# Attention stage of a two-layer decoder step: rotation of gathered query rows by pairs of tiles, sinks as a score column, half the keys for the first block

## The chip, the cores and the metric

The kernel runs on one core of a Trainium2 chip. The metric is the device time of one launch, in microseconds. Three runs of the kernel before took 1693.32, 1693.46 and 1696.6 us, with a median of 1693.46 us.

## What is computed

One inference step of a two-layer decoder, for a prompt of 512 tokens and 8 single-token samples (520 columns together), with a width of 1024, in float32. Each layer is a half-weighted SwiGLU, a token mixer, and a second half-weighted SwiGLU. The mixer of layer 0 is a pooling mixer. The mixer of layer 1, which the change touches, is sliding-window attention with 16 query heads, 4 key heads and a head width of 64. The first 16 rows of each head are rotated by position, and each head has a sink, a score that takes part in the softmax but has no value. Cut to what matters:

```
def _rope(x, pos):                       # first 16 of the 64 rows of a head
    out = concat([x1 * cos - x2 * sin, x2 * cos + x1 * sin, x[..., 16:]])

def _sink_attention(q, k, v, mask, sinks):
    s = einsum(q, k) * HEAD_DIM ** -0.5
    s = where(mask, s, -inf)             # 0 <= d < 128 and key position >= 0
    m = maximum(max(s), sink)
    p = exp(s - m)
    denom = sum(p) + exp(sink - m)
    return einsum(p / denom, v)
```

## The kernel before

**Tiling.** Activations stand with the width on partitions (8 tiles of 128) and the 520 tokens along the free axis. Float32 products are made from a high and a low float32r part: each product takes three matmuls (`terms`, L410), of 260 columns each. The parts are made by `split` (L241: a ScalarE copy to the high part, a VectorE subtraction to the low one), and for weights in `Weights._split` (L194 and L195). Weights are loaded on SyncE's DMA queue in chunks of up to 1 MB, into 3 rotating buffers (`raw`).

**The attention stage** (L1033 to L1341). There are 8 query tiles t. Each holds two heads, on partitions 0 to 63 (e = 0) and 64 to 127 (e = 1). A tile is projected in two halves of 24 matmuls (`q_part`, `q_half`, line L417 in the profile). `q_evac` (L1056) then rotates it in `rope` (L914): a ScalarE copy out of PSUM (L919) and four VectorE operations on 128x520 (L920 to L923), of which only 16 of each 64 partitions change; the others are multiplied by a table of ones and zeros. A split follows, and two small copies (L1063) take the samples' columns to `qz`.

The attention of a tile is two `Unit`s, for query blocks (0, 1) and (2, 3), so there are 16 units. A unit has four parts, one for each block and head:

- `scores` (L1073): 12 matmuls, scores against two blocks of keys, 256 columns. Block 0 has no block of keys before it, and its second 128 columns are masked out whole.
- `softmax` (L1090): a VectorE operation that adds the mask and takes the row maximum (L1101) for each part; three small ones that scale the maximum and join the sink (L1115 to L1117); ScalarE's exponentials with a sum (L1121), one more for the sink (L1129); the sum and its reciprocal (L1130, L1131); and the four scalings, two on ScalarE (L1134), two on VectorE (L1136).
- `turn` (L1138): transposes on TensorE (L1146) and a split into float32r parts.
- `values` (L1156): 9 or 12 matmuls (L1169) and two ScalarE copies to `oT` (L1181).

**Order.** The loop at L1313 writes scores of unit n, then a projection part, then turn of unit n - 2 (LAG), other jobs, softmax of unit n, values of unit n - 3 (VLAG), then evacuations. The scheduler of the framework may move instructions on an engine; those marked `later` keep their place. Each engine works through its own queue in order. PSUM has four double banks (`duo`), in which projections, scores, transposes and values take turns. Score tiles `sm` exist for three units at a time: units 2, 5, 8 and so on use the memory of the keys (`kT`), the others have their own. From n = 8, the samples' attention (L1219, L1254) and the first halves of the output projection (`o_part`, L417) are among the jobs. Loads of the output weights `w_o` and of `vc` (the cached values, 1 MB, L1296) stand in SyncE's queue among the rest; GpSimd has one small DMA into `vc` (L1297).

Of the kernel before, what the change touches and what calls it, by code (L numbers as in the profile page):

```python
# [18 lines left out]
P = 128  # L19
D = 1024  # L20
KT = 8
# [24 lines left out]
C_END = C_AB + 2  # L46
# [7 lines left out]
def shape_constants():  # L54
    c = np.zeros((P, C_END), np.float32)
    q = np.arange(P)[:, None]
    j = np.arange(256)[None, :]
    ok = (j > q) & (j <= q + P)
    c[:, C_MASK : C_MASK + 256] = np.where(j <= q, 0.0, NEG)
    c[:, C_MASK + 256 : C_MASK + 512] = np.where(ok, 0.0, NEG)  # L60
    pos = np.concatenate([np.arange(SP), np.full(NS, PAST)]).astype(np.float32)
    inv = np.power(500000.0, -np.arange(8) * (2.0 / 16)).astype(np.float32)
    ang = (inv[:, None] * pos[None, :]).astype(np.float32).astype(np.float64)
    cos, sin = np.cos(ang), np.sin(ang)
    c[:, C_COS : C_COS + TOK] = 1.0
    for h in (0, 64):
        c[h : h + 8, C_COS : C_COS + TOK] = cos
        c[h + 8 : h + 16, C_COS : C_COS + TOK] = cos
        c[h : h + 8, C_SIN : C_SIN + TOK] = -sin
        c[h + 8 : h + 16, C_SIN : C_SIN + TOK] = sin  # L70
    for gi, w in enumerate(WINS):
# [141 lines left out]
def yoco_step(ctx, tc, ins, outs):  # L213
# [694 lines left out]
    kT = [kvp.tile([P, TOK], F32, tag="kT", name=f"kT{g}", bufs=2) for g in range(2)]  # L908
# [124 lines left out]
    with tc.tile_pool(name="at", bufs=2) as at:  # L1033
# [3 lines left out]
        nc.scalar.dma_start(csq.rearrange("p a t -> p (a t)"), consts[:, C_COS : C_COS + 2 * TOK])  # L1037
# [6 lines left out]

        r8 = at.tile([P, NB], F32, name="r8", bufs=1)
        nr8 = at.tile([P, NB, 2], F32, name="nr8", bufs=1)
        oS = at.tile([P, KT, NS], F32, name="oS", bufs=1)
        oT = [big.tile([P, SP], F32, tag="th", name="oT") for t in range(KT)]
# [6 lines left out]

        def q_evac(t, banks):  # L1056
            qT = at.tile([P, TOK], F32, tag="qT", name="qT", bufs=1)
            rope(qT, banks, cosq, sinq, at, ("rp0", "rp1"))
            qq = pair(XX, [P, SP])
            split(qq, qT[:, :SP])  # L1060
            for e in range(2):
                rows = slice(e * 64, e * 64 + 64)
                V.tensor_copy(qz[t // 4][rows, e, t % 4, :], qT[rows, SP:])  # L1063
            return qq

        class Unit:
# [6 lines left out]
            def scores(self):  # L1073
# [5 lines left out]
                for bi, b in enumerate(self.bs):  # L1079
                    for e in range(2):  # L1080
# [4 lines left out]
                        kc_ = slice(k0, k0 + 256)  # L1085
# [4 lines left out]
            def softmax(self):  # L1090
                c0 = self.t * 8 + self.h * 4
                mx, nm, es, den = (at.tile([P, 4], F32, tag=n, name=n) for n in ("mx", "nm", "es", "den"))
                self.sms = []
                for bi, b in enumerate(self.bs):
                    if (2 * self.t + self.h) % 3 < 2:
                        sm = at.tile([P, 512], F32, tag="sm", name="sm", bufs=4)
                    else:
                        sm = kvp.tile([P, TOK], F32, tag="kT", name="sm", bufs=2)
                    mk = C_MASK if b == 0 else C_MASK + 256
                    for e in range(2):  # L1100
                        ins = V.tensor_tensor_reduce(  # L1101
                            out=sm[:, e * 256 : (e + 1) * 256],
                            in0=self.pe[e][:, bi * 256 : (bi + 1) * 256],
                            in1=cst[:, mk : mk + 256],
                            op0=ALU.add,
                            op1=ALU.max,
                            scale=1.0,
                            scalar=NEG,
                            accum_out=mx[:, bi * 2 + e : bi * 2 + e + 1],
                        )  # L1110
                        if self.t == 0:
                            later(ins)
                    self.sms.append(sm)
                nr = nr8[:, self.bs[0] : self.bs[1] + 1, :].rearrange("p b e -> p (b e)")
                later(V.tensor_tensor(nm, mx, nr, op=ALU.mult))  # L1115
                later(V.tensor_tensor(nm, nm, nsinks[:, c0 : c0 + 4], op=ALU.min))
                V.tensor_tensor(es, sinks[:, c0 : c0 + 4], nm, op=ALU.add)  # L1117
                part = lambda i: self.sms[i // 2][:, (i % 2) * 256 : (i % 2) * 256 + 256]
                for i in range(4):
                    b = self.bs[i // 2]  # L1120
                    S.activation(  # L1121
                        part(i),
                        part(i),
                        AF.Exp,
                        scale=r8[:, b : b + 1],
                        bias=nm[:, i : i + 1],
                        accum_out=den[:, i : i + 1],
                    )
                S.activation(es, es, AF.Exp)  # L1129
                V.tensor_tensor(den, den, es, op=ALU.add)  # L1130
                V.reciprocal(den, den)  # L1131
                for i in range(4):
                    if i % 2:
                        S.activation(part(i), part(i), AF.Copy, scale=den[:, i : i + 1])  # L1134
                    else:
                        V.tensor_scalar(part(i), part(i), den[:, i : i + 1], None, op0=ALU.mult)  # L1136

            def turn(self):  # L1138
                self.pts = []
                both = duo()  # L1140
                for bi, b in enumerate(self.bs):
                    kts = (0,) if b == 0 else (0, 1)
                    pt = both[:, bi, :]
                    for kt in kts:
                        for e in range(2):
                            T.transpose(  # L1146
                                pt[:, kt * 256 + e * P : kt * 256 + (e + 1) * P],
                                self.sms[bi][:, e * 256 + kt * P : e * 256 + (kt + 1) * P],
# [7 lines left out]
            def values(self):  # L1156
# [20 lines left out]
                po3 = po.rearrange("p (b e q) -> p b e q", b=2, e=2)  # L1177
                for e in range(2):
# [15 lines left out]
        qq[0] = q_evac(0, qb[0])  # L1194
        rstd_tok()
        q_part(1, 0)
        V.tensor_scalar(r8, r_tok[:, :NB], 0.125, None, op0=ALU.mult)
        V.tensor_scalar(nr8, r_tok[:, :NB].unsqueeze(2).broadcast_to([P, NB, 2]), -0.125, None, op0=ALU.mult)
        q_part(1, 1)
        rstd_samples()  # L1200
        rs8 = at.tile([P, NS], F32, name="rs8", bufs=1)
        V.tensor_scalar(rs8, R[:, SP:], 0.125, None, op0=ALU.mult)
        q_part(2, 0)
# [109 lines left out]
        for n in range(2 * KT + VLAG):  # L1313
            if n < 2 * KT:
                units[n].scores()
            for part in q_parts.get(n, ()):
                q_part(*part)
# [6 lines left out]
            if n >= VLAG:  # L1324
                units[n - VLAG].values()
            if n in q_evacs:
                qq[q_evacs[n]] = q_evac(q_evacs[n], qb[q_evacs[n]])
# [125 lines left out]
```

## Time and profile before

| | |
|---|---|
| median of three runs | 1693.46 us |
| the profiled execution | 1691.85 us |
| its span in the profile | 1690.0 us |
| TensorE matmul busy | 1657.5 us, 98% |
| VectorE, ScalarE, GpSimd busy | 74%, 53%, 8% |
| mean granted TensorE clock | 0.992 |
| attention stage, 1150 to 1295 us: VectorE, ScalarE busy | 113.06 and 107.58 of 145 us |

The profile shows one execution. "Busy" is the time in which an engine had an instruction; times between brackets are idle times of an engine, with what ended them. Matmuls overlap their weight loads and one another, so that the duration of one is more than the step from one to the next. The granted clock says what part of full speed TensorE was given in a stretch. The values of units 4, 8, 12 and 15 (L1169) begin at 1214.72, 1244.40, 1275.75 and 1292.79 us; marks like these divide the stage in the text on the prediction.

### The profile page before, as it was taken

The numbers are of one execution on the slowest core, as the hardware profiler recorded it, in microseconds if no ns is written. First come the engines' busy times: TensorE is split into PE (matmuls) and PEld (weight loads), VectorE is DVE, ScalarE is ACT, GpSimd is POOL, SyncE is SP. The second block draws the span as 40 slices with busy tenths as digits, with TensorE's granted clock in tenths as the row PEclk, the third lists the DMA queues.
The fourth block names the chain that finished last, engine by engine and source line by source line (L and its number), as shares of the span: only waits on it lengthen the run. The fifth ranks groups of instructions, "written<-read, shape, count | busy, mean of one in ns | idle before, by whom it ended". The sixth has DMA issues, their size and how long they took to land.

```text
span 1690.0 us, 34449 instructions
## 1 busy us (share of the span) xinstructions
PE 1657.5 (98%) x13754; PEld 1642.7 (97%) x13754; DVE 1254.4 (74%) x2452; ACT 903.5 (53%) x1793; POOL 142.3 (8%) x176
## 2 busy tenths in 40 slices
PE   9999999999999999999999999999989999999997
PEld 8999999999999999999999999998879999999996
DVE  6866866887875875888775875888876885785776
ACT  6743643665652652656552652655886653463454
POOL 0101101000101101100101101100000100110100
PEclk9999999999999999999999999999899999999998
DMA  8546745652545855634745845642122554674631
GB/s 214 137 128 142 181 134 136 174 167 80 129 140 129 178 147 130 153 117 129 162 137 125 187 137 127 152 138 71 50 51 76 131 137 131 148 173 132 148 109 52
DMA packets 313327, 224.71 MB, mean 133 GB/s; under 512 B 9152, under 2 KB 289320, under 8 KB 313126
## 3 DMA queue, kind: packets, MB, share of 16 engines
q1 hardware_dynamic: 286416, 176.13, 36.8%
q0 software_dynamic: 22432, 40.26, 14.5%
q10 hardware_dynamic: 4318, 6.12, 1.2%
q8 instruction: 108, 1.77, 0.4%
q14 instruction: 53, 0.43, 0.1%
HBM read 180.11 MB, written 5.04 MB: 110 GB/s over the span
## 4 chain that ended last, share of the span: by engine, by line
PE 90%; DVE 4%; ACT 3%; DMA 1%; issue 1%; DVEq 0%; ACTq 0%
PE ps L443 45%; PE ps L417 41%; ACT sm L1121 1%; PE ps L1169 1%; PE ps L814 1%; DVE wl L195 1%; DMA pr<-in_bands_dram 1%; PE ps L839 1%; DVE sm L1101 1%; DVE xl L246 0%; ACT wh L194 0%; PE ps L1146 0%; PE ps L381 0%; PE ps L698 0%; DMA pr<-in_pool_w_dram 0%
## 5 line engine op out<-in xcount | busy, mean ns | idle before, releaser
L194 ACT ACTIVATE wh<-raw 128x512 fp32r<-128x512 f32 (+1 forms) x736 | 446.3, 621 | 544.8 <-PE ps L417 329.5
L195 DVE TENSOR_TENSOR wl<-raw,wh 128x512 fp32r<-128x512 f32 (+1 forms) x736 | 486.9, 676 | 200.7 <-ACT wh L194 197.2
L443 PE MATMUL ps<-th,wh 128*128 128x260 f32 x1216 | 343.7, 283 | 0.0
L443 PE MATMUL ps<-tl,wh 128*128 128x260 f32 x1216 | 343.1, 282 | 0.0
L443 PE MATMUL ps<-th,wl 128*128 128x260 f32 x1216 | 341.5, 282 | 0.0
L417 PE MATMUL ps<-hh,wh 128*128 128x260 f32 x1376 | 284.3, 285 | 2.3 <-DVE mx L1101 1.0
L417 PE MATMUL ps<-hl,wh 128*128 128x260 f32 x1376 | 283.2, 283 | 0.0
L417 PE MATMUL ps<-hh,wl 128*128 128x260 f32 x1376 | 280.7, 282 | 0.0
L443 PEld LDWEIGHTS ps<-tl,wh 128*128 128x128 f32 x1216 | 229.0, 188 | 0.0
L443 PEld LDWEIGHTS ps<-th,wh 128*128 128x128 f32 x1216 | 228.7, 188 | 0.2 <-ACT sa L523 0.2
L443 PEld LDWEIGHTS ps<-th,wl 128*128 128x128 f32 x1216 | 228.1, 188 | 0.0
L417 PEld LDWEIGHTS ps<-hh,wh 128*128 128x128 f32 x1376 | 213.5, 189 | 4.0 <-DVE mx L1101 1.2
L417 PEld LDWEIGHTS ps<-hl,wh 128*128 128x128 f32 x1376 | 215.2, 189 | 0.1
L417 PEld LDWEIGHTS ps<-hh,wl 128*128 128x128 f32 x1376 | 214.0, 189 | 0.0
L443 PE MATMUL ps<-xh,wh 128*128 128x260 f32 x672 | 188.3, 283 | 0.0
L443 PE MATMUL ps<-xl,wh 128*128 128x260 f32 x672 | 188.2, 283 | 0.0
L443 PE MATMUL ps<-xh,wl 128*128 128x260 f32 x672 | 184.2, 282 | 0.0
L159 POOL DMA_DIRECT2D raw<-raw x76 | 65.5, 862 | 1302.8 <-DMA raw<-in_ffn_w_up_dram 438.9
L417 PE MATMUL ps<-xh,wh 128*128 128x260 f32 x736 | 149.4, 285 | 0.6 <-ACT wh L194 0.6
L417 PE MATMUL ps<-xl,wh 128*128 128x260 f32 x736 | 149.5, 284 | 0.5 <-DVE xl L717 0.5
L417 PE MATMUL ps<-xh,wl 128*128 128x260 f32 x736 | 147.8, 283 | 0.1
L591 DVE TENSOR_TENSOR u<-ps,R 128x520 f32<-128x520 f32 (+1 forms) x99 | 67.2, 681 | 106.3 <-PE ps L417 106.3
(260 smaller groups left out, 2849.1 us busy)
## 6 DMA issues: line engine op xcount, KB each, us to landing
raw<-in_ffn_w_gate_dram SPq DMA_DIRECT2D x87, 512.0 KB, 3.9
raw<-in_ffn_w_up_dram SPq DMA_DIRECT2D x87, 512.0 KB, 5.4
raw<-in_ffn_w_down_dram SPq DMA_DIRECT2D x32, 1024.0 KB, 5.3
raw<-raw POOLq DMA_DIRECT2D x76, 256.0 KB, 3.3
S<-in_ffn_w_up_dram SPq DMA_DIRECT2D x76, 256.0 KB, 5.6
S<-raw POOLq DMA_DIRECT2D x76, 256.0 KB, 4.7
raw<-in_ffn_w_down_dram SPq DMA_DIRECT2D x16, 768.0 KB, 4.9
raw<-in_w_q_dram SPq DMA_DIRECT2D x8, 512.0 KB, 4.0
```

The costliest lines, as they stand in the source:

```text
L159: G.dma_start(blk(raw, 2, 1), blk(raw, 1, 1), accum_op=ALU.add)
L194: self.pin(nc.scalar.activation(dh, src, AF.Copy))
L195: self.pin(nc.vector.tensor_tensor(dl, src, dh.bitcast(F32), op=ALU.subtract))
L417: ins = T.matmul(banks[:, hf, :H], a[:, kk, :], hcols(b, hf), start=(first and i == 0), stop=(last and i == 2),)
L443: T.matmul(bank[:, :H], a[:, kk, :], b, start=(not more and kk == 0 and i == 0), stop=(kk == 3 and i == 2), skip_group_check=more,)
L591: V.tensor_tensor(parts(u), bank[:, hfs[0] : hfs[-1] + 1, :H], parts(R[:, c]), op=ALU.mult)
L814: T.matmul(o, a[:, s], b[:, kk, :], start=(n == 0), stop=(n == 5))
L839: T.matmul(po[:, half * 256 : half * 256 + 256], z[:, tau, c], b, start=(i == 0), stop=(i == len(lst) - 1),)
L1101: ins = V.tensor_tensor_reduce(out=sm[:, e * 256 : (e + 1) * 256], in0=self.pe[e][:, bi * 256 : (bi + 1) * 256], in1=cst[:, mk : mk + 256] ...
L1121: S.activation(part(i), part(i), AF.Exp, scale=r8[:, b : b + 1], bias=nm[:, i : i + 1], accum_out=den[:, i : i + 1],)
L1169: T.matmul(po[:, bi * 256 : (bi + 1) * 256], a, p_[:, kc_], start=(n == 0), stop=(n == 3 * len(kts) - 1),)
```

## The change

1. **Rotation by pairs.** `q_evac` copies a projected tile to SBUF (`qraw`), and two DMAs on SyncE's queue gather its 2 x 16 rows to be rotated into a 64-row tile `qG`, which takes two query tiles. `q_turn` rotates these 64 rows at once, and four DMAs put them back: two on SyncE's queue (e = 0), two on GpSimd's (e = 1). `q_split` then splits a tile, and the samples' copies go to GpSimd. Tiles 0 to 3 are projected before the first scores; turns and splits have places of their own in the loop.
2. **Sinks as a column.** The scores are scaled by minus the row's norm factor in the VectorE operation that adds the mask, whose running minimum begins at minus the sink. A column that holds minus the sink stands behind the scores (written by GpSimd, two small copies for a unit), so that the exponential's own sum has the sink in it. The three small operations, the sink's exponential and the addition go. Three scalings of four are on VectorE, one on ScalarE.
3. **Half the keys.** For block 0, scores, mask, exponential and scaling work on 128 columns.

`oT` tiles are taken one by one from the buffers that `qraw` had. The constants get two more tables. In the built programs, TensorE has the same number of matmuls, in the same order up to the end of tile 1's projection and again from the second half of the output projection on; the other engines differ between tile 0's evacuation and there, but for a few places on GpSimd's queue.

```diff
-    kT = [kvp.tile([P, TOK], F32, tag="kT", name=f"kT{g}", bufs=2) for g in range(2)]
+    kT2 = kvp.tile([P, 2, TOK], F32, tag="kT", name="kT")
+    kT = [kT2[:, g, :] for g in range(2)]
...
         def q_evac(t, banks):
-            qT = at.tile([P, TOK], F32, tag="qT", name="qT", bufs=1)
-            rope(qT, banks, cosq, sinq, at, ("rp0", "rp1"))
-            qq = pair(XX, [P, SP])
-            split(qq, qT[:, :SP])
+            qraw[t] = big.tile([P, TOK], F32, tag="th", name="qraw")
+            later(S.copy(halves(qraw[t]), banks[:, :, :H]))
+            if t % 2 == 0:
+                turned[t // 2] = at.tile([64, TOK], F32, tag="qT", name="qG", bufs=1)
+            for e, rows in enumerate(strips(qraw[t])):
+                o = t % 2 * 32 + e * 16
+                nc.sync.dma_start(turned[t // 2][o : o + 16, :], rows)
+
+        def q_turn(s):
+            G = turned[s]
+            sw = at.tile([64, TOK], F32, tag="rp1", name="rp1", bufs=1)
+            V.stream_shuffle(sw, G, swap16)
+            V.tensor_tensor(G, G, cosq[:64], op=ALU.mult)
+            V.tensor_tensor(sw, sw, sinq[:64], op=ALU.mult)
+            V.tensor_tensor(G, G, sw, op=ALU.add)
+            for t in (2 * s, 2 * s + 1):
+                for e, rows in enumerate(strips(qraw[t])):
+                    o = t % 2 * 32 + e * 16
+                    if e:
+                        nc.gpsimd.dma_start(rows, G[o : o + 16, :])
+                    else:
+                        nc.sync.dma_start(rows, G[o : o + 16, :])
+
+        def q_split(t):
+            qq[t] = pair(XX, [P, SP])
+            split(qq[t], qraw[t][:, :SP])
             for e in range(2):
                 rows = slice(e * 64, e * 64 + 64)
-                V.tensor_copy(qz[t // 4][rows, e, t % 4, :], qT[rows, SP:])
-            return qq
+                nc.gpsimd.tensor_copy(qz[t // 4][rows, e, t % 4, :], qraw[t][rows, SP:])
...
-                        kc_ = slice(k0, k0 + 256)
+                        kc_ = slice(k0, k0 + (256 if b else P))
+                        o = o[:, : 256 if b else P]
...
+                ns = [256 if b else P for b in self.bs]
+                self.sms = [sm[:, i // 2, (i % 2) * 260 : (i % 2) * 260 + ns[i // 2] + 1] for i in range(4)]
+                for bi, n in enumerate(ns):
+                    dst = sm[:, bi, :].rearrange("p (e c) -> p e c", e=2)[:, :, n]
+                    nc.gpsimd.tensor_copy(dst, nsinks[:, c0 + 2 * bi : c0 + 2 * bi + 2])
                 for i in range(4):
-                    b = self.bs[i // 2]
+                    bi, e = i // 2, i % 2
+                    b, n = self.bs[bi], ns[bi]
+                    mk = C_MASK + 256 if b else C_MASK
+                    ins = V.tensor_tensor_reduce(
+                        out=self.sms[i][:, :n],
+                        in0=self.pe[e][:, bi * 256 : bi * 256 + n],
+                        in1=cst[:, mk : mk + n],
+                        op0=ALU.add,
+                        op1=ALU.min,
+                        scale=nr8[:, b : b + 1],
+                        scalar=nsinks[:, c0 + i : c0 + i + 1],
+                        accum_out=nm[:, i : i + 1],
+                    )
+                for i in range(4):
                     S.activation(
-                        part(i),
...
+                        self.sms[i], self.sms[i], AF.Exp, scale=-1.0, bias=nm[:, i : i + 1], accum_out=den[:, i : i + 1]
                     )
-                S.activation(es, es, AF.Exp)
-                V.tensor_tensor(den, den, es, op=ALU.add)
                 V.reciprocal(den, den)
                 for i in range(4):
-                    if i % 2:
-                        S.activation(part(i), part(i), AF.Copy, scale=den[:, i : i + 1])
+                    p_ = self.sms[i][:, : ns[i // 2]]
+                    if i == 3:
+                        S.activation(p_, p_, AF.Copy, scale=den[:, i : i + 1])
                     else:
-                        V.tensor_scalar(part(i), part(i), den[:, i : i + 1], None, op0=ALU.mult)
+                        V.tensor_scalar(p_, p_, den[:, i : i + 1], None, op0=ALU.mult)
...
-        q_parts = {0: [(2, 1)], 1: [(3, 0)], 2: [(3, 1), (4, 0)], 3: [(4, 1)]}
-        q_evacs = {0: 1, 1: 2, 3: 3, 4: 4}
-        for t in range(5, KT):
-            q_parts[2 * t - 6], q_parts[2 * t - 5] = [(t, 0)], [(t, 1)]
-            q_evacs[2 * t - 5] = t
+        for h in (0, 1):
+            q_part(2, h)
+        q_turn(0)
+        q_part(3, 0)
+        q_evac(2, qb[2])
+        q_part(3, 1)
+        q_split(0)
+        q_split(1)
+        q_evac(3, qb[3])
+        q_parts = {n: (4 + n // 2, n % 2) for n in range(8)}
+        q_evacs = {1: 4, 3: 5, 5: 6, 7: 7}
+        q_turns = {1: 1, 5: 2, 8: 3}
+        q_splits = {2: (2,), 3: (3,), 6: (4,), 7: (5,), 9: (6, 7)}
```

More of the change, by code (lines that the diff above doesn't have):

```diff
@@ L45 @@
 C_AB = C_SEL + 32
-C_END = C_AB + 2
+C_CG = C_AB + 2
+C_SG = C_CG + TOK
+C_END = C_SG + TOK
 B_G = 0
@@ L70, in shape_constants @@
         c[h + 8 : h + 16, C_SIN : C_SIN + TOK] = sin
+    for h in range(0, P, 16):
+        c[h : h + 8, C_CG : C_CG + TOK] = cos
+        c[h + 8 : h + 16, C_CG : C_CG + TOK] = cos
+        c[h : h + 8, C_SG : C_SG + TOK] = -sin
+        c[h + 8 : h + 16, C_SG : C_SG + TOK] = sin
     for gi, w in enumerate(WINS):
@@ L1042, in yoco_step @@
             nc.gpsimd.memset(qz[g], 0.0)
-        r8 = at.tile([P, NB], F32, name="r8", bufs=1)
-        nr8 = at.tile([P, NB, 2], F32, name="nr8", bufs=1)
+        nr8 = at.tile([P, NB], F32, name="nr8", bufs=1)
         oS = at.tile([P, KT, NS], F32, name="oS", bufs=1)
-        oT = [big.tile([P, SP], F32, tag="th", name="oT") for t in range(KT)]
+        oT, qraw = [], {}
         def q_half(banks, k0):
@@ L1091, in softmax @@
                 c0 = self.t * 8 + self.h * 4
[L1092 to L1113, printed above, removed]
@@ L1129, in softmax @@
-                S.activation(es, es, AF.Exp)
-                V.tensor_tensor(den, den, es, op=ALU.add)
+                nm, den = (at.tile([P, 4], F32, tag=n, name=n) for n in ("nm", "den"))
+                pool = at if (2 * self.t + self.h) % 3 < 2 else kvp
+                sm = pool.tile([P, 2, TOK], F32, tag="sm" if pool is at else "kT", name="sm")
+                ns = [256 if b else P for b in self.bs]
+                self.sms = [sm[:, i // 2, (i % 2) * 260 : (i % 2) * 260 + ns[i // 2] + 1] for i in range(4)]
@@ L1315, in yoco_step @@
                 units[n].scores()
-            for part in q_parts.get(n, ()):
-                q_part(*part)
+            if n in q_parts:
+                q_part(*q_parts[n])
             if LAG <= n < 2 * KT + LAG:
```

35 lines of the change are left out of this document (18 added, 17 removed).

## The prediction

> **What bounds the kernel now.** I read the busy table and the slices first: TensorE is busy 98% of the span, with one dip, in the slices of the attention stage. The windows of that stage show what can be won. Columns: stretch, its length, then busy time and instructions of PE, PEld, DVE, ACT, POOL, then granted clock, DMA share, GB/s.
>
> ```profile
> 1150.00:1170.00 20.00, 19.95 (x172) 18.80 (x172) 16.77 (x59) 6.79 (x12) 0.00 (x0) 1.00 0.24 62
> 1170.00:1200.00 30.00, 25.30 (x180) 22.96 (x179) 21.74 (x87) 24.64 (x74) 0.00 (x0) 0.83 0.22 49
> 1200.00:1250.00 50.00, 43.57 (x356) 39.03 (x356) 43.35 (x169) 42.55 (x120) 0.52 (x1) 0.97 0.16 44
> 1250.00:1295.00 45.00, 43.40 (x372) 41.68 (x371) 31.21 (x102) 33.60 (x96) 0.00 (x0) 1.00 0.29 71
> ```
>
> The reader is to see that TensorE idles 145 - 132.2 = 12.8 us, nearly all from 1170 to 1250, where VectorE and ScalarE are both busy some 85%. The timeline of TensorE shows the two largest gaps, and what they do to its clock:
>
> ```profile
> 1181.99 0.48 PE L1169 MATMUL ps<-xh,tl 128*128 128x256 f32 x2 [2.48 <-ACT xh L245]
> ...
> 1187.38 0.80 PE L1169 MATMUL ps<-xh,tl 128*128 128x256 f32 x2 [2.03 <-ACT xh L245]
> ...
> 1189.12 0.64 PE L417 MATMUL ps<-hh,wh 128*128 128x260 f32 x2
> ```
>
> After a gap of 2.48 us, matmuls step by some 0.21 us in place of 0.12, until 1193.1: 8.7 us of work at a little over half speed, a loss of 3.8 us. So at most 12.8 + 3.8, some 17 us, can be won here; outside this stage the queues' order is unchanged. The groups by form in 1150 to 1295 price the operations:
>
> ```profile
> L1121 ACT ACTIVATE sm<-sm,nm,r 128x256 f32<-128x256 f32 x64 | 37.6, 590 | 4.8 <-DVE nm L1116 4.7
> L1101 DVE CUSTOM_DVE_ANT_0 sm<-ps,cst 128x256 f32<-128x256 f32 x64 | 24.0, 419 | 7.9 <-PE ps L1146 4.1 <-PE ps L1088 3.6
> L1134 ACT ACTIVATE sm<-sm,den 128x256 f32<-128x256 f32 x32 | 14.4, 500 | 2.2 <-DVE nm L1116 1.1 <-DVE den L1131 1.0
> L1136 DVE TENSOR_SCALAR sm<-sm,den 128x256 f32<-128x256 f32 x32 | 9.8, 348 | 0.2
> L921 DVE STREAM_SHUFFLE rp<-rp 128x520 f32<-128x520 f32 x8 | 5.9, 740 | 0.0
> L246 DVE TENSOR_TENSOR xl<-ps,xh 128x256 fp32r<-128x256 f32 x8 | 3.4, 419 | 0.6 <-ACT xh L245 0.6
> L1129 ACT ACTIVATE es<-es 128x4 f32<-128x4 f32 x16 | 3.0, 190 | 0.0
> L1130 DVE TENSOR_TENSOR den<-den,es 128x4 f32<-128x4 f32 x16 | 2.6, 160 | 7.5 <-ACT es L1129 7.4
> ```
>
> **The change, part by part.** *VectorE.* The four rotation operations (691, 740, 694, 698 ns, together 2.82 us) run 4 times in place of 8: -11.3 us, if 64 partitions cost as much as 128 (no reason for less). The small ones, 16 x (157 + 157 + 156 + 160) ns: -10.1. The copies to `qz`, 16 x 166 ns, go to GpSimd: -2.7. Halved columns: a subtraction costs 685 ns for 512 columns and 419 for 256, about 1.04 ns a column, so 128 columns save 133 ns; 16 mask operations: -2.1. Scalings: 32 full ones become 32 full and 16 half ones (348 - 133 = 215 ns): +3.4. Sum -22.8 of 113.1 us.
>
> *ScalarE.* 16 scalings fewer, 16 x 500: -8.0. The sink's exponentials: -3.0. Halved exponentials: 592 against 373 ns for splits of 512 and 256 columns gives 0.86 ns a column, 16 x 110 ns: -1.8. Sum -12.8 of 107.6.
>
> *TensorE.* 48 score matmuls have half the columns. Two run side by side (the rows of e = 0 and 1) every 0.115 us, so 24 such steps save between 0 (if the weight load, 194 ns, sets the step) and 24 x 0.058 = 1.4 us. I take 0.7, in the middle, as both rows are near.
>
> *What is added.* 24 DMA issues on SP (16 gathers, 8 put-backs), 0.37 to 0.58 us each by SP's timeline; 8 on POOL (518 to 862 ns); 48 small POOL copies, for which the nearest row is a memset of 128x64 at 151 ns. Each DMA moves 16 rows of 2,080 bytes, 33 KB. Nearest rows for the landing:
>
> ```profile
> raw<-raw POOLq DMA_DIRECT2D x76, 256.0 KB, 3.3
> ...
> raw<-in_w_o_dram SPq DMA_DIRECT2D x8, 512.0 KB, 5.3
> ...
> sink_s<-in_attn_sinks_dram SPq DMA_DIRECT2D x8, 0.1 KB, 8.6
> ...
> kc<-knew POOLq DMA_DIRECT2D x4, 2.0 KB, 1.8
> out_dram<-hrow POOLq DMA_DIRECT2D x2, 30.0 KB, 1.9
> ```
>
> I take 2.0 us on a quiet queue (30 KB: 1.9), with 1.8 and 8.6 as ends; the 8.6 us stand behind two 1 MB copies on the same queue.
>
> *Where it lies: the start.* Before, a tile is ready 0.57 + 2.82 + 1.31 = 4.7 us after its projection at best. Now it takes 0.57 (copy) + 1.0 (two issues) + 2.0 + 2.8 + 0.5 + 2.0 + 1.3 (split) = 10.2 us. What hides this at first is the projection of tiles 2 and 3: 96 matmuls at 119.6 ns, 11.5 us, from the end of tile 1 (1155.6) to 1167.2. With tile 1 copied at 1156.7, gathers land at 1159.3, the VectorE chain (with one weight split in it) ends at 1162.4, tile 0 is back at 1165.2 and split at 1166.5: 0.7 us before scores of unit 0 are due. If this cover fails, each us late is a us.
>
> The put-back of tile 1 on SP stands behind a 1 MB load of `w_o`, issued at 1163.1, so I let it land with that, at 1170. ScalarE's split of tile 1 waits for it, and in ScalarE's queue the first exponentials are behind. VectorE's pass for unit 0 thus begins at 1171.3, 8 us later than before (1163.1), while exponentials begin at 1171.7 against 1170.58. After that VectorE waits until 1174.3 for the gather of tile 3 (its copy is behind the same ScalarE wait), with the pass of unit 1 behind it. Following the queues with the rows' durations, unit 0's transposes come at 1180 (before 1177.0), and its values at 1188.7, after a gap of 3 us (before 1187.4, after two). At the half clock this costs 2.6 us again.
>
> *On to unit 4.* Here a unit has 5.5 us of VectorE, 6.1 of ScalarE and 6.3 of TensorE (24 projection matmuls, 2.87, among them), and with the gaps between them the queues give 6.55 us a unit; with waits of 1.5 us for sink columns that stand behind put-backs in POOL's queue, values of unit 4 begin at 1218, 3.3 us later than before. But by then all 8 tiles are projected; before, tile 7 was not (48 matmuls, 5.7 us). **Lead: 2.4 us.**
>
> *Units 4 to 8.* Before: 1244.40 - 1214.72 = 29.7, less the 5.7 for tile 7: 24.0. After: ScalarE has per unit 2.25 (exponentials at their step of 0.59, or 0.48) + 0.5 + 1.08 (split of transposes) + 0.73 (`oT`) + 0.31 + 0.58 (query copy and split), 5.45; four units 21.8. VectorE has 4.8 a unit (masks 1.29, scalings 0.8, reciprocal 0.2, splits 1.7, rotation 0.62, samples 0.2), TensorE 4.35 (scores 1.1, transposes 1.0, values 1.4, samples 0.85). **Lead: 2.2 us more**, less if the third pair waits behind the 1 MB of `vc`, which I put at 0.7 us: 1.5.
>
> *Units 8 to 12.* Before 31.4; TensorE's own work there is 28.9 (four units of 3.5, 32 sample matmuls at 0.106, 96 output matmuls at 0.12). ScalarE needs 18.8. Of the 2.5 us of stall I take away 1.9. *From there* to the end TensorE is full already. With the 0.7 of halved scores: 2.4 + 1.5 + 1.9 + 0.7 = **6.5 us.** Against the execution's 1691.85 this gives 1685.4; against the median 1693.46, which is 1.6 above that execution, **1687.0 us**.
>
> [...]
>
> **The rivals.**
>
> *All of it is won.* If landings are quick, and the 3 us gap at unit 0 closes, the stage loses neither that nor the clock: 6.5 + 3 + 2.6 = 12, 1681. For it: VectorE falls to 90 of 145 us. Against it: the chain above, which is queue order and not load.
>
> [...]
>
> *The waits eat the gain.* Put-backs and gathers stand at the heads of ScalarE's and POOL's queues in four places; 1.5 us more at each is 6 us: 1693. For it: both engines work in order.
>
> *Slower: put-backs behind bulk loads.* At tile 1 (behind `w_o`) and at tiles 6 and 7 (behind `vc`), the wait holds up all exponentials. I have 5.5 us for these landings. If they take 10.5 us (one row has 8.6), the loss is 2 x 5 and 2.6 of half clock, 12.6 us: 6.1 slower, 1699.5. From 8.7 us on, without the clock, nothing is left of the gain. Against it: the loads are 1 MB, and 512 KB land in 5.3.
>
> That the halved keys bring nothing is in the sum (0 to 1.4).
>
> **How the numbers follow.** Forecast 45% (1683.5 to 1690), all won 12%, GpSimd 8%, waits 15%, slower 20%. 0.2% is 3.4 us, about what a measurement of this kernel can tell from no change: faster 45 + 12 = 57%, same 8 + 15 = 23%, slower 20%. The range, 1680 to 1698, takes in both middle rivals, half of "all won", and slower by up to 4.5 us; about 18% are left out.
>
> **What would show it.** Scores of unit 0 near 1167 us; VectorE at about 90 and ScalarE at about 95 us in the stage; values of unit 4 after all projections, near 1218; the time between units 4 and 8 below 23 us. Wrong: TensorE waiting for `xh` from `qraw` before the first scores, exponentials waiting for POOL copies above 0.5 us each time, or put-backs that land later than 6 us.

## The result, and the profile after

The changed kernel takes **1698.57 us** (median of 22 runs, 1694.81 to 1704.32); the kernel before takes 1693.38 us beside it (22 runs, 1691.31 to 1698.96). The ratio is **1.0025, 95% interval 1.0017 to 1.0033**: slower by 4.2 us, where 6.5 us of gain were forecast. The profiled execution has a span of 1693.4 us (before: 1690.0) and a mean granted clock of 0.988 (before: 0.992).

The stage in the same four windows as before (columns as there):

```profile
1150.00:1170.00 20.00, 20.00 (x169) 19.52 (x168) 9.22 (x24) 6.94 (x12) 2.03 (x5) 1.00 0.39 94
1170.00:1200.00 30.00, 26.01 (x201) 23.69 (x201) 23.59 (x80) 20.62 (x64) 2.50 (x11) 0.89 0.23 50
1200.00:1250.00 50.00, 42.06 (x324) 37.83 (x321) 39.09 (x127) 36.57 (x109) 6.81 (x27) 0.87 0.20 51
1250.00:1295.00 45.00, 43.65 (x346) 41.55 (x346) 30.41 (x94) 27.86 (x80) 1.43 (x8) 0.92 0.28 71
```

VectorE has 10.8 us less to do in these 145 us, ScalarE 15.6 us less (part of both is other work that moved over the edges). Summed over the four rows VectorE is busy 102.3 us and ScalarE 92.0; the prediction had about 90 and 95. TensorE idles 13.3 us, before 12.8: the idle time stayed. New is the column of the clock: 0.87 and 0.92 from 1200 on, where it was 0.97 and 1.00.

TensorE's timeline has the marks that the prediction used, the first matmul of the values of units 4, 8, 12 and 15:

```profile
1218.27 0.51 PE L1196 MATMUL ps<-xh,tl 128*128 128x256 f32 x2 [0.52 <-DVE nm L1141]
...
1245.98 0.48 PE L1196 MATMUL ps<-xh,tl 128*128 128x256 f32 x2
...
1280.70 0.40 PE L1196 MATMUL ps<-xh,tl 128*128 128x256 f32 x2
...
1297.70 0.40 PE L1196 MATMUL ps<-xh,tl 128*128 128x256 f32 x2
```

Unit 4 comes at 1218.27, forecast 1218. From unit 4 to 8 it takes 27.7 us (forecast 22.5), from 8 to 12 34.7 us (forecast 29.5), and from 12 to 15 17.0, as before. So the loss is made between units 4 and 12. At unit 15 the changed kernel is 4.9 us late; the rest of this execution then ran 1.5 us shorter than that of the kernel before, so that the spans differ by 3.4.

**What happens there.** I cut the stretch at the edges at which the granted clock changes. They lie on a grid of 3.41 us. After, columns as above:

```profile
1219.66:1223.07 3.41, 1.72 (x18) 1.28 (x18) 3.38 (x13) 3.35 (x10) 0.33 (x2) 1.00 0.00 0
1223.07:1226.49 3.42, 3.31 (x15) 3.34 (x16) 1.95 (x7) 2.50 (x10) 0.00 (x0) 0.50 0.11 24
1226.49:1229.90 3.41, 3.41 (x22) 2.96 (x21) 2.78 (x8) 1.37 (x3) 0.00 (x0) 0.50 0.00 0
1229.90:1233.31 3.41, 2.02 (x19) 1.93 (x18) 3.41 (x11) 2.92 (x9) 1.62 (x4) 1.00 0.69 206
1233.31:1236.73 3.42, 3.42 (x22) 2.97 (x21) 1.74 (x7) 1.49 (x5) 0.87 (x3) 0.50 0.43 141
1243.55:1246.96 3.41, 1.07 (x9) 1.07 (x10) 3.41 (x15) 2.71 (x10) 0.00 (x0) 1.00 0.00 0
1246.96:1250.37 3.41, 3.41 (x19) 2.54 (x17) 1.20 (x6) 1.64 (x7) 0.18 (x2) 0.50 0.02 5
```

A window in which TensorE was idle for 1.4 to 2.3 us (the first, fourth and sixth row) is followed by one or two at half clock, and in those TensorE is busy nearly from end to end: 1.7 us lost in each. Between the marks of units 4 and 12 there are six half-clock windows, 10.2 us: these five (the fifth is at 1250.37) and one at 1257.2, which follows a window with only 0.2 us idle. Before, the same units had one (the last row):

```profile
1230.20:1233.61 3.41, 2.42 (x24) 1.95 (x23) 3.41 (x10) 1.77 (x5) 0.00 (x0) 1.00 0.00 0
1233.61:1237.02 3.41, 1.56 (x13) 1.27 (x11) 2.58 (x15) 3.28 (x11) 0.00 (x0) 1.00 0.46 135
1237.02:1240.44 3.42, 3.06 (x14) 2.83 (x16) 2.68 (x11) 2.54 (x8) 0.00 (x0) 0.50 0.88 175
```

Take the lost clock off, and the forecast is met: units 4 to 8 have three half-clock windows, 27.7 - 5.1 = 22.6 (forecast 22.5); units 8 to 12 have three, 34.7 - 5.1 = 29.6 (forecast 29.5).

For units 4 to 8 this closeness is in part luck. The prediction set out from the 24.0 us of the kernel before, which hold a half-clock window themselves; at full clock they are 22.3, so that the change gains nothing there. It took ScalarE for the limit, with 21.8 us, and had 4 x 4.8 = 19.2 for VectorE; from unit 4 to 8 ScalarE is busy 21.5 us and VectorE 22.8.

The gaps of TensorE that lie in the three windows with much idle time have three different names:

```profile
1223.18 1.84 PE L1255 MATMUL ps<-qz,kc 128*128 128x8 f32 x8 [1.63 <-ACT qraw L1072]
...
1232.84 0.51 PE L1196 MATMUL ps<-xh,tl 128*128 128x256 f32 x2 [1.39 <-DVE nm L1141]
...
1245.89 0.33 PE L1268 MATMUL ps<-ident,sT 128*128 128x128 f32 x1 [2.45 <-DVE sT L1258]
```

ScalarE's copy of a projected tile, a mask operation, and VectorE's operation on the samples' scores end them. So no single wait makes the loss. What the three windows share is VectorE, busy 3.38 to 3.41 of their 3.41 us, though over the stage it has time to spare. In the longest gap the operation on the samples' scores (L1258) stood in VectorE's queue behind four mask operations and a split, from 1243.19 to 1245.66.

**A ledger of the clock.** Each execution has its span and its mean granted clock. Span x clock is what it would take at full clock, if TensorE were the bound in every half-clock window; the rest is what the clock took. Of that rest, 4.6 us before and 4.8 after (in the profiled executions) lie behind the last matmul (it ends at 1679.0 and 1683.4 us), where the clock holds up nothing, so only differences of it tell. Over 22 runs the changed kernel has 1674.3 + 22.0 us, the kernel before 1676.2 + 16.1 (29 runs): counted so, the change gained 1.9 us at full clock and lost 5.9 by the clock. That takes each us of the clock for a us of time. Among the 29 runs of the kernel before, only about 0.7 us of span come with each; at that rate the 5.9 us are 4.1 us of time, which is all of the 4.0 us between the mean spans, and nothing is gained at full clock. So the gain lies between 0 and 1.9 us, and the clock's loss covers the slowdown either way. The table under the experiments has the same for every kernel.

### The profile page after: what moved, and what is told of

It is laid out like the page before. It is cut to its first block, busy times and chain, and to the rows that moved or that the text cites. A ratio compares the mean times of both kernels' runs of the same rounds, so it can differ in the third digit from the quotient of the medians.

```text
span 1693.4 us, 34499 instructions
## 1 busy us (share of the span) xinstructions
PE 1661.6 (98%) x13754; PEld 1647.4 (97%) x13754; DVE 1245.3 (74%) x2367; ACT 889.9 (53%) x1761; POOL 155.8 (9%) x232
## 3 DMA queue, kind: packets, MB, share of 16 engines
q0 software_dynamic: 22688, 40.53, 14.6%
## 4 chain that ended last, share of the span: by engine, by line
PE 91%; DVE 3%; ACT 2%; DMA 2%; issue 1%; SPq 0%; ACTq 0%; DVEq 0%
PE ps L450 45%; PE ps L424 41%; PE ps L1196 1%; PE ps L821 1%; DMA pr<-in_bands_dram 1%; DVE sm L1141 1%; PE ps L846 1%; DMA qraw<-qG 0%; PE ps L1173 0%; ACT sm L1154 0%; DVE wl L202 0%; DMA qG<-qraw 0%; PE ps L388 0%; PE ps L1122 0%; PE ps L705 0%
```

## The experiments

First theories. *Mask*: the mask operation got dearer, and with it the way to the values. *Fill*: with all tiles projected early, TensorE has too little to do between a unit's scores and its values in units 4 to 12.

**soft**: the new softmax and the halved keys, on the old rotation and order (against the changed kernel).

```diff
-            later(S.copy(halves(qraw[t]), banks[:, :, :H]))
+            rope(qT, banks, cosq, sinq, at, ("rp0", "rp1"))
...
-        q_parts = {n: (4 + n // 2, n % 2) for n in range(8)}
+        q_parts = {0: [(2, 1)], 1: [(3, 0)], 2: [(3, 1), (4, 0)], 3: [(4, 1)]}
```

> The kernel before with the second and third part of the change (sink column, fused mask operation, half keys), and the old rotation and order of projections. Theory 'mask' (the mask operation with two column operands costs 118 ns more, 64 times, 7.6 us of VectorE on the way from scores to values, and eats the gain): no faster than before, 1693 to 1697. Theory 'fill' (all projections are done before unit 4, so the waits of units 4 to 12 have no TensorE work in them, and the clock falls): the loss comes with the order of projections, so this one gains, 1687 to 1690.

Ratio 1.0004 (0.999 to 1.0018). *Mask* had this. The new softmax alone gains nothing.

**rot**: the new rotation and order, on the old softmax with full keys (against the changed kernel).

```diff
-                        scale=nr8[:, b : b + 1],
-                        scalar=nsinks[:, c0 + i : c0 + i + 1],
+                        scale=1.0,
+                        scalar=NEG,
...
+                S.activation(es, es, AF.Exp)
+                V.tensor_tensor(den, den, es, op=ALU.add)
```

> The changed kernel with the old softmax and full keys: the first part of the change alone. 'Mask': the mask operation is the old one, so this is faster than before, 1687 to 1691. 'Fill': the early projections are here, so this one is slower than before, 1697 to 1702.

Ratio 1.0042 (1.0026 to 1.0058): +7 us, as *fill* had it.

**half**: the kernel before with halved keys alone.

```diff
-                        kc_ = slice(k0, k0 + 256)
+                        kc_ = slice(k0, k0 + (256 if b else P))
```

> The kernel before with 128 keys for block 0, nothing else. VectorE 16 x 133 ns and ScalarE 16 x (110 + 2 half scalings) less, TensorE 0 to 1.4 us. Both theories: 1 to 2 us faster than before, about 1692.

Ratio 0.9999 (0.999 to 1.0009). The 0 to 1.4 us of the forecast can't be told from nothing, and the 1 to 2 us that both theories expected aren't seen.

**imm**: the changed kernel, mask operation with constants.

```diff
-                        scale=nr8[:, b : b + 1],
-                        scalar=nsinks[:, c0 + i : c0 + i + 1],
+                        scale=-0.125,
+                        scalar=-NEG,
```

> The changed kernel with constants in place of the two column operands of the mask operation: it leaves out the row's norm factor in the scores and the sink in the maximum. 'Mask': the operation falls from 537 to about 419 ns, and the time falls by 5 us or more against the changed kernel, to 1693 or below. 'Fill': the operation gets as much shorter, but the time falls by 2 us at most, to about 1696.

Ratio 1.0009 (0.9997 to 1.0022). 2.7 of the 4.2 us come back, between both theories (the intervals of the two kernels overlap). By the table below it is the clock that comes back: it takes 17.9 us here and 22.0 in the changed kernel. In the groups by form, the operation in the changed kernel

```profile
L1141 DVE CUSTOM_DVE_ANT_0 sm<-ps,cst,nsinks 128x256 f32<-128x256 f32 x48 | 23.6, 537 | 4.9 <-PE ps L1124 3.3 <-PE ps L1173 1.4
L1141 DVE CUSTOM_DVE_ANT_0 sm<-ps,cst,nsinks 128x128 f32<-128x128 f32 x16 | 5.9, 405 | 8.8 <-PE ps L1124 4.2 <-PE ps L1173 2.4 <-POOL qz L1099 2.2
```

and in imm:

```profile
L1141 DVE CUSTOM_DVE_ANT_0 sm<-ps,cst 128x256 f32<-128x256 f32 x48 | 17.9, 418 | 4.6 <-PE ps L1124 3.3 <-PE ps L1173 1.2
```

The two column operands cost 119 ns an instruction. The start of one mask operation to the next takes 0.465 us with them and 0.345 without. But imm, with 98.1 us of VectorE in 1150 to 1300 against 114.0 before, is still not faster than before.

**immscale**: one of the two columns taken away.

> The changed kernel with a constant as scale of the mask operation (the row's norm factor is left out of the scores), the start still a column. It only asks which operand makes the operation 118 ns dearer: about 478 ns if each column costs half, 419 if it is the scale, 537 if it is the start.

A single execution took 1699.88 us. The operation takes

```profile
L1141 DVE CUSTOM_DVE_ANT_0 sm<-ps,cst,nsinks 128x256 f32<-128x256 f32 x48 | 20.8, 479 | 3.9 <-PE ps L1124 2.0 <-PE ps L1173 1.8
```

479 ns: each column costs some 60.

**early**: soft, in the early order of projections, still without rotation DMAs.

```diff
-        q_parts = {0: [(2, 1)], 1: [(3, 0)], 2: [(3, 1), (4, 0)], 3: [(4, 1)]}
+        q_parts = {n: [(4 + n // 2, n % 2)] for n in range(8)}
+        q_evacs = {1: 4, 3: 5, 5: 6, 7: 7}
...
```

> The run soft (column of sinks and half keys on the old rotation), with one thing changed: the projections in the early order of the changed kernel, tiles 2 and 3 before the first scores and tile 7 by unit 7. There are no rotation DMAs. Theory 'order': this carries the loss, 1698 to 1702, as in the run with the new rotation alone (1700.3), and the granted clock after unit 4 falls. Theory 'queue waits': 1694 to 1696, as soft (1695.1).

Ratio 1.0035 (1.0023 to 1.0047): 5 us above soft, as *order* (the former *fill*) had it. DMA waits aren't needed for the loss. By the table, most of these 5 us aren't the clock's: early has 4.0 us more than soft at full clock and 0.7 more by the clock. So in this pair the waits themselves cost time: in the profiled executions TensorE idles 16.6 us in 1150 to 1300, and 11.5 in soft's.

**spread2**: the changed kernel, projections spread as before the change; the turn and split of tiles 6 and 7 and the samples' second scores come two units later for it.

```diff
-        q_parts = {n: (4 + n // 2, n % 2) for n in range(8)}
-        q_evacs = {1: 4, 3: 5, 5: 6, 7: 7}
-        q_turns = {1: 1, 5: 2, 8: 3}
-        q_splits = {2: (2,), 3: (3,), 6: (4,), 7: (5,), 9: (6, 7)}
+        q_parts = {0: (4, 0), 1: (4, 1), 3: (5, 0), 4: (5, 1), 6: (6, 0), 7: (6, 1), 8: (7, 0), 9: (7, 1)}
+        q_evacs = {1: 4, 4: 5, 7: 6, 9: 7}
+        q_turns = {1: 1, 5: 2, 10: 3}
+        q_splits = {2: (2,), 3: (3,), 6: (4,), 7: (5,), 11: (6, 7)}
...
```

> The changed kernel with tiles 5 to 7 projected later (tile 7 in the iterations of units 8 and 9, as before the change), its pair turned at 10, split at 11, the samples' second scores at 12. Theory 'order': the new kernel has spent its projections by unit 4, so that TensorE has nothing to do in the gaps of units 4 to 12 and loses its clock there. Then 3 to 5 us of the 5 lost come back, 1693.5 to 1695.5, with the granted clock of 1215 to 1280 at 0.95 or more. Theory 'queue waits': what costs is gathers and put-backs at the heads of the engines' queues, and these are only moved closer to their users: 1698 to 1701, with TensorE waiting for the splits of tiles 6 and 7 before unit 12.

Ratio 1.007 (1.0055 to 1.0086), worse than either had it. Unit 2's iteration has no projection now, and a gap of 4.85 us opens at 1181.6, ended by a weight split on ScalarE. So it doesn't test the late units cleanly.

**cheap**: soft, with constants in the mask operation and the norm factor in the exponential.

```diff
-                        scale=nr8[:, b : b + 1],
-                        scalar=nsinks[:, c0 + i : c0 + i + 1],
+                        scale=1.0,
+                        scalar=NEG,
...
+                later(V.tensor_tensor(nm, mx, nr, op=ALU.mult))
+                later(V.tensor_tensor(nm, nm, nsinks[:, c0 : c0 + 4], op=ALU.min))
```

> The run soft with the mask operation of before (constants for scale and start), the norm factor in the exponential, and the sink column divided by it in advance; two of the three small operations stay. VectorE saves 64 x 118 ns = 7.6 us and pays 32 x 157 ns = 5.0 us against soft. If the path goes through the mask operation (it is what frees the bank that the values wait for), 1691.5 to 1694, below soft by 1.5 to 3. If VectorE's time is off the path here, as the run soft suggested, 1694.5 to 1696.

Ratio 1.0017 (1.0006 to 1.0027). VectorE has 4.9 us less than in soft (111.4 against 116.3 in 1150 to 1300), and the kernel isn't faster; its median of 1697.65 us lies above both ranges.

**vcnew**: GpSimd's small copy into the cached values, issued later.

```diff
-            nc.gpsimd.dma_start(vc[0][0:1], vnew)
...
+            if n == 10:
+                nc.gpsimd.dma_start(vc[0][0:1], vnew)
```

> The changed kernel with one DMA moved: GpSimd's small copy into the cached values, which waits 3.6 us for their 1 MB load at 1232, is issued at unit 10 and not at 4. Theory 'queue waits': put-backs and sink columns of units 7 and 8 are no longer behind it, the mask operation of unit 8 doesn't wait, and 1.5 to 3 us come back: 1695.5 to 1697. Theory 'order': TensorE has no work to put there either way, 1698 to 1699.

Ratio 1.0026 (1.0015 to 1.0038), as the changed kernel. In the changed kernel a mask operation at 1237.28 had waited 2.20 us for GpSimd's copies behind that one; in vcnew this wait is gone and the time is the same. No cost of it can be seen.

**keepA, keepS, keepB**: matmuls that do nothing, to hold the clock up.

```diff
+        none = at.tile([P, P], F32R, name="none", bufs=1)
+        V.tensor_scalar(none, ident, 0.0, None, op0=ALU.mult)
...
+                    T.matmul(
+                        qb[t][:, i % 2, :H], none, kk[1][0][:, :H], start=False, stop=stop and i >= count - 2
+                    )
```

> The changed kernel with 48 matmuls added that multiply by zero weights, into projection banks that are open anyway, just ahead of the values of units 0 to 4 (16, then 8 each; some 5.7 us of TensorE work, in the gaps of 1223 and before as far as it fits). They change no result. Theory 'clock': the loss is the granted clock. It halves for windows of 3.4 us, 1.7 us of loss each, after any such window with more than about 1.5 us of TensorE idle; matmuls that do nothing keep the windows busy, the mean clock goes from 0.987 to 0.989 or more, and the time falls, 1693 to 1697. Theory 'stall': the loss is the waiting as such, the clock is only its shadow, and added work can only delay: 1699 to 1704.

> The run soft with 56 such matmuls, 8 ahead of the values of each of units 0 to 6 (6.7 us of work). Theory 'clock': soft has 1673 us of work at full clock against 1676 of the kernel before, and loses 20 us by the clock against 16; with the clock kept up, 1690 to 1693.5, the first below the kernel before. Theory 'stall': 1696 to 1701.

> The kernel before with the same 56 matmuls. Theory 'clock': it has three of its four slow windows ahead of the first of them, so at most one is saved, 1.7 us, and work that doesn't fit a gap is added: 1692 to 1697. Theory 'stall': all 6.7 us that don't lie in a gap are paid, 1695 to 1700.

Ratios 1.0049 (1.0032 to 1.0066), 1.0065 (1.0047 to 1.0083), 1.0102 (1.0084 to 1.012); keepA is where *stall* had it, the others above both. *Clock*, as I put it, falls: the filling brought no slow window away (21.7 us lost in keepA, 22.0 without) and 4.5 us were paid at full clock. In the timeline of keepA the gap ahead of unit 0's values is still 2.3 us long. My reading, which no run isolates: what is filled in ahead also delays the scores behind it, and with them what the next gap waits for. Idle time of TensorE wasn't free room here; it moved along with the work.

**bankA, bankS, bankB**: PSUM banks dealt out by hand.

```diff
-                pe = duo()
+                pe = bank_of("s2" if n > 7 and n % 2 else "s")
...
-                both = duo()
+                both = bank_of("t")
...
-                po = ps()
+                po = value_bank()
...
```

> The changed kernel with the PSUM banks dealt out by hand from unit 4 to 11: one double bank for scores, one for transposes, one for projections, and the two halves of the fourth for values and the samples. Values no longer take a double bank each, and so no longer wait for the mask operation of a later unit to give one back (11.4 us of TensorE's waits in the changed kernel are of this kind). Theory 'banks': 4 to 6 us come back, 1692.5 to 1695, with the granted clock of 1215 to 1280 above 0.93. Theory 'chain': the bank is only the first thing that is late; behind it the values' own split or the next scores are as late, since a unit has less TensorE work between its scores and its values than the other engines need: 1697 to 1700, and the waits have other names.

> The run soft (old rotation and order, new softmax) with the same dealing of banks from unit 6 to 11. Theory 'banks': 2 to 4 us below soft, 1690.5 to 1693, better than the kernel before. Theory 'chain': 1694 to 1697.

> The kernel before with the same dealing of banks from unit 6 to 11. It has 2.2 us of waits of this kind. Theory 'banks': 1691.5 to 1693.5. Theory 'chain': 1693 to 1696.

Ratios 1.009 (1.0071 to 1.0109), 1.0021 (1.0006 to 1.0036), 1.0065 (1.0048 to 1.0082). In the waits view (total us, times, longest) of 1150 to 1295 the largest wait of TensorE's matmuls in the changed kernel was

```profile
PE ps L1196 <- DVE nm L1141: 6.5, 6, 2.5
```

The 11.4 us of the expectation add 4.9 us to it that weight loads wait, in the same gaps. In bankA, 2.5 us of the 6.5 are left, and the waits have other names, on transposes (L1189) above all:

```profile
PE ps L1189 <- DVE xl L253: 4.5, 2, 3.7
PE ps L1212 <- DVE nm L1157: 2.5, 1, 2.5
```

*Banks* falls, for this dealing. That the times lie above *chain* too suggests that my dealing took away freedom that the ring of four gives; no run separates the two.

**order, first, tile7**: the kernel before, with its projections moved and nothing else. The added lines are those of order, first and tile7; in the first two, tiles 2 and 3 stand ahead of the loop.

```diff
-        q_parts = {0: [(2, 1)], 1: [(3, 0)], 2: [(3, 1), (4, 0)], 3: [(4, 1)]}
+        q_parts = {n: [(4 + n // 2, n % 2)] for n in range(8)}
...
+        q_parts = {n: [(3 + n // 2, n % 2)] for n in range(2, 10)}
...
+        q_parts[6], q_parts[7] = [(6, 0), (6, 1)], [(7, 0), (7, 1)]
+        del q_parts[8], q_parts[9]
```

> The kernel before, with old rotation and softmax, and only its projections in the early order of the changed kernel (tiles 2 and 3 ahead of the first scores, tile 7 by unit 7). Theory 'order': an iteration with a projection part has 2.9 us of TensorE work between a unit's scores and the values that follow; without it the other engines' chain lies open. Then order alone costs 4 to 7 us, 1697.5 to 1700.5, near the run rot (1700.3), and the DMA rotation with all its VectorE saving is worth about nothing in it. Rival 'rotation': the order is harmless without the new softmax, 1693 to 1695, and rot's loss is the DMA rotation's.

> The kernel before, with only tiles 2 and 3 projected ahead of the first scores; tiles 4 to 7 as before, in units 2 to 9, so that units 0 and 1 have no projection. If the loss arises where iterations stand without a part, it is paid here at units 0 and 1: 1696 to 1699. If only the late units (4 to 12) count, 1693 to 1695.

> The kernel before, with only tile 7 projected earlier (in unit 7's iteration, tile 6 in unit 6's), so that units 8 and 9 have no projection. Theory 'order': 1696 to 1699, TensorE idle in 1240 to 1265. Otherwise 1693 to 1695.

Ratios 0.9998 (0.9987 to 1.0009), 1.0049 (1.0036 to 1.0063), 1.0021 (1.0009 to 1.0033). The early order by itself shows no cost: *order* falls as a cause of its own. tile7's time agrees with *order*, but not its trace: in 1240 to 1265 TensorE idles 2.4 us, less than the 3.2 before, and the granted clock is 0.72 in place of 0.99. first lies above both ranges (1704.13 us). It has a gap of 5.8 us at 1192, and three half-clock windows more than the kernel before by 1202; so units without a projection part can lose at the start of the loop too.

**All of it in one table** (without immscale, a single execution). "At full clock" is the mean of span x clock, "clock" the mean of the rest.

| kernel | ratio to before | at full clock, us | clock, us |
|---|---|---|---|
| before | 1 | 1676.2 | 16.1 |
| half | 0.9999 | 1674.5 | 17.3 |
| order | 0.9998 | 1674.5 | 18.1 |
| imm | 1.0009 | 1675.5 | 17.9 |
| soft | 1.0004 | 1673.0 | 20.2 |
| cheap | 1.0017 | 1675.1 | 21.1 |
| bankS | 1.0021 | 1672.0 | 23.7 |
| tile7 | 1.0021 | 1673.8 | 22.8 |
| **after** | **1.0025** | **1674.3** | **22.0** |
| vcnew | 1.0026 | 1675.2 | 22.4 |
| early | 1.0035 | 1677.0 | 20.9 |
| rot | 1.0042 | 1676.4 | 22.9 |
| first | 1.0049 | 1676.7 | 24.7 |
| spread2 | 1.007 | 1676.1 | 29.0 |
| bankA | 1.009 | 1676.6 | 30.7 |
| bankB | 1.0065 | 1678.6 | 24.1 |
| keepA, keepS, keepB | 1.0049 to 1.0102 | 1678.8 to 1685.1 | 21.3 to 24.8 |

Leaving aside the kernels with added matmuls, the time at full clock spreads over 6.6 us (1672.0 to 1678.6), what the clock takes over 14.6 us. So most of what sets these kernels apart is the clock's, but not all of it: early, cheap and bankB differ from the kernels that they are made of by 2 to 4 us at full clock. The same holds among runs of one program: the 29 runs of the kernel before go from 1689.3 us at a clock of 0.993 to 1696.9 at 0.988, about 0.7 us of span for each us that the clock takes.

Three parts of the change against one another: new softmax on the old order +0.04%, on the early order (early against order) +0.37%; DMA rotation on the old softmax (rot against order) +0.44%, on the new one (after against early) -0.10%. The effects don't add. No part carries the loss in every combination. Shorter mask operations take 4.1 of the clock's 5.9 us away in the changed kernel (imm) and none in soft (cheap).

**What is shown and what stays open.** Shown: the loss arises between units 4 and 12; in the profiled execution it is six half-clock windows against one (ahead of unit 4 it is two against three), five of them in the wake of a window with 1.4 us or more of TensorE idle; by the ledger, what the clock takes is enough for all of the slowdown, and at full clock the changed kernel isn't slower. Not settled: why this arrangement makes longer gaps in more windows at the same total of idle time, and whether the clock could be held up, since my filling also delayed the work. None of these kernels beats the kernel before by more than its interval.

## Why the prediction was wrong

- **VectorE, -22.8 us.** By the rows it is -14.6, and by the busy time of the whole run, which counts overlapping instructions once, -9.1 (1254.4 to 1245.3). Rotation -11.5 (forecast -11.3), small operations -9.8 (-10.1), `qz` -2.6 (-2.7), scalings +3.8 (+3.4) hold. The mask operation was mis-sized: +5.5 (24.0 to 29.5) in place of -2.1, as I took a column for as cheap as a constant. The cost of a 64-row operation was right: the shuffle takes 740 ns in both.

```profile
L1082 DVE STREAM_SHUFFLE rp<-qG 64x520 f32<-64x520 f32 x4 | 3.0, 740 | 0.0
L1163 DVE TENSOR_SCALAR sm<-sm,den 128x128 f32<-128x128 f32 x16 | 3.8, 279 | 0.2
```

  The halved scaling is dearer than extrapolated, 279 ns for 215.
- **ScalarE, -12.8.** Busy time of the whole run fell by 13.6.
- **Landings of 2.0 us, and later behind bulk loads.** Right in the numbers. In the DMA view (count, KB, median us to landing):

```profile
qG<-qraw SPq DMA_DIRECT2D x16, 32.5 KB, 1.9
qraw<-qG SPq DMA_DIRECT2D x8, 32.5 KB, 6.7
qraw<-qG POOLq DMA_DIRECT2D x8, 32.5 KB, 1.8
```

  For SP's put-backs only one landing is known, tile 1's, issued at 1164.46 behind the loads of `w_o` and landed 6.65 us later at 1171.1 (forecast 1170). That is over the 6 us that the prediction named as a sign of being wrong, and yet the start held. That it would land with the load ahead of it was my estimate, and no run shows that the queue made it wait: tile 1's put-back on GpSimd's own queue, issued at 1163.40 beside the same loads, took 5.13 us, and tile 6's and 7's beside `vc` 4.52 and 4.18; the other five on that queue took 1.8. The row of 8.6 us, on which the slow rival leaned, is the middle of two known landings, 1.59 and 15.58 us.
- **The start, up to unit 4.** Right: first scores at 1167.0 (1167.2), transposes of unit 0 at 1180.7 (1180), its values at 1189.3 (1188.7) behind a gap of 2.5 us with the clock halved, unit 4 at 1218.27 (1218). Of the lead of 2.2 us there, 1.7 is one half-clock window less (two from 1188.9 on, before three from 1182.4 on) (the prediction put 3.8 us of half clock before and 2.6 after).
- **Units 4 to 8 and 8 to 12: the steps that failed.** Both sums were made at full clock, by the busiest engine and TensorE's own work. I charged the half clock behind unit 0's gap, 2.6 us, and none after it. 10.2 us of it came between units 4 and 12, before only 1.7. Without it both sums are met within 0.1 us, for units 4 to 8 partly by luck, as said above. The prediction had even shown this at 1182, in its own second fence (after 2.48 us idle, steps of 0.21 us in place of 0.12), and not asked where else the change would leave gaps of that size.
- **After unit 12.** Right, 17.0 us as before.
- **Halved scores, 0.7.** Not seen: half gives a ratio of 0.9999 (0.999 to 1.0009).
- **The rivals.** For GpSimd (8%), it is its own copies that came late. Of the 48 small ones (most near 186 ns) six took 349 to 656 ns; each of these began under a VectorE operation with two SBUF inputs and ended within 0.05 us of its end. VectorE's rows didn't grow: a split of 512 columns takes 684 ns (685 before), a scaling 347 (348). So no cost to VectorE can be seen. "The waits eat the gain" and "put-backs behind bulk loads" come near in time, but not in their mechanism: the start was on schedule, and vcnew took one later wait away at no gain.

## What to carry to other kernels

Where TensorE is busy in most of a stage, sum it at full clock first, then lay the 3.41 us windows over it and look for those with more than 1.3 us of idle time. Here 57 of 62 such windows were followed by a stretch at half clock; a stretch had 1.8 windows on average, each worth up to 1.7 us. This is a lower bound, as 30 of the 87 stretches began after less idle time. So idle time that gathered in one window cost more here than the same time spread over several (of 567 windows with less than 0.8 us, 14 were followed by a half-clock one). Relieving another engine by itself won nothing over the kernel before: in imm, VectorE had 98 us in this stage against 114. So look at how full an engine is just ahead of a gap, and not only at its share of the stage. The parts of this change didn't add, so each is to be measured in its own combination.

## What the hardware showed that I had not expected

**The clock follows single windows.** In the 20 profiles of this case I laid the grid of 3.413 us over 1150 to 1300; the edges of the clock fit it to 0.07 us (root mean square) or better in each. Windows at full clock with 1.75 us or more of TensorE idle were followed by a half-clock one in 39 of 39 cases, with 1.3 to 1.75 us in 18 of 23, with 0.8 to 1.3 us in 16 of 54, with less in 14 of 567. Once at half clock, 0.8 us of idle held it there in 29 of 29 cases, less in 40 of 127. These bounds were read off the same profiles, so they describe this kernel and its variants. The grid isn't tied to the start of the program: counted from the start of the span, its first edge from 1150 us on lies between 1150.0 (vcnew) and 1153.2 (immscale), at 1151.7 in the kernel before and 1151.4 in the changed one. So a gap may fall in one window or be cut in two; that this makes the 7.6 us between runs of one program is my reading, which no run isolates.

**Column operands in the fused mask operation** cost 60 ns each (418, 479 and 537 ns with none, one and two of them, 256 columns).
